# First scale and shift by quarters, and five products begun instead of three, in a decoder step of two layers

## The chip, the cores and the metric

One core of one Trainium2 chip. The metric is the device time of one execution in microseconds (us), the median of several runs. In the texts PE is TensorE, DVE is VectorE, ACT is ScalarE, POOL is GpSimd and SP is SyncE, which issues most DMAs.

## The reference, cut to what matters

Two layers of a decoder run for a prompt of 256 tokens and for 8 sample sequences of 4 tokens, 288 token columns in all, 1024 features. Each sub-layer starts with an RMSNorm that is scaled and shifted by vectors which a large product (`w_ada`) makes of a condition vector `c`:

```python
mod = cs @ p['w_ada'][l] + p['b_ada'][l]              # cs = silu(c), 1024 x 6144 weights a layer
sh1, sc1, g1, sh2, sc2, g2 = jnp.split(mod, 6, axis=-1)
xn = xf * lax.rsqrt(jnp.mean(xf * xf, axis=-1, keepdims=True) + EPS) * g
h = xn * (1.0 + scale[:, None, :]) + shift[:, None, :]
...
proj = jnp.einsum('btd,de->bte', h, w_in)             # retention: q, k, v, gate
q = rope(heads(q, RET_DK), pos0); k = rope(heads(k, RET_DK), pos0) * RET_DK ** -0.5
```

So nothing of the first layer's large product `h @ w_in` can start before `sh1` and `sc1`, that is before 8 MB of `w_ada` have arrived and been multiplied. All is float32; a product of the projections is made of three passes over weights and activations that are split into a high part and a low rest (`hi*hi`, `hi*lo`, `lo*hi`).

## The kernel before, in words

Features lie on partitions, tokens on columns; the 1024 features are 8 tiles of 128 (`KT`). Weights stream from memory in blocks of 128x1024 (512 KB) through SP's queue in the order that `plan_weights` writes down (L308); a block can be fetched when a place of its pool is free. A block of the projections is split on its way: ACT writes its high part (`whi`, L416), DVE the rest (`wlo`, L417), at most `LOOK` = 2 blocks ahead. A block of `w_ada` is used unsplit, by `ada_step` (L449): four matmuls of 32 columns of the array each. One output tile of the projection, called a product here, is 24 matmuls of 128x288 (3 passes times 8 feature tiles, `product`, L528). PE, DVE, ACT, POOL and SP each run a fixed order of instructions, which a scheduling layer makes when the program is built; an instruction that waits holds all that stand behind it on its engine.

The first phase is `first_h` (L659). `w_ada`'s first two chunks (`ada(0)`, `ada(1)`, 8 blocks each) are laid out so that the first chunk gives scale and shift of feature tiles 0 to 3 and the second of tiles 4 to 7. After the first chunk `modulated` (L612) makes h of tiles 0 to 3: on DVE scale times norm weight (`am`), the sample columns (`hs`, three steps), the prompt columns (`h`), on ACT the high part (`hh`, L637 and L646), on DVE the rest of the prompt columns (`hl`, L648). Then the first `EARLY` = 3 products are begun over tiles 0 to 3 (PSUM tiles `pe`), the second chunk's blocks lying between their weight blocks; when it is done, h of tiles 4 to 7 is made, and the three products are ended. Only then does `retention` go on: rotary positions on DVE (`rt`, L744 to L748) read the first four products, and the other products follow. The first phase has 8 places for blocks of its own (`RAW_START`) beside 4 common ones.

Constants of the first phase are fetched by ACT's queue: `cst_a` (cosines and sines, 288 KB), `cst_r` (902 KB), `cst_b`, `prm_b`. Each is held back by a copy of one column on POOL (`load_cst`, L521) that reads a scale or shift vector.

```python
            self.product(*begun[-1], KT, 0, P, h, 0, KT // 2)
        ...
        for i, (p, w) in enumerate(begun):
            if i == FREE:
                self.hold = False
            self.product(p, w, KT, 0, P, h, KT // 2)
```

## Time and profile before, and how to read them

| | |
|---|---|
| median of 3 runs | 1219.81 us (1219.09 to 1222.64) |
| the profiled execution's own time | 1217.6 us |
| its span in the profile | 1215.8 us |
| PE busy | 1150.0 us, 95% of the span |
| DVE, ACT, POOL busy | 872.7, 609.1, 316.2 us |
| DMA | 269 MB, mean 221 GB/s |
| granted PE clock, mean | 0.982 |

The profile shows one execution. The views used are: the page (busy time by engine), busy time by stretch with the granted clock and DMA, who waited for whom, and the timeline of one engine, whose rows give start, duration, engine, line, operation and, in brackets, an idle time and what ended it. A matmul on plain float32 operands shows as two records, one of the split parts as one; the rows of a timeline merge records of one form that follow each other, and the last record's drain is part of a row's duration, so that the pace is read from start to start.

### The profile page before, as it was taken

The page shows a single profiled execution, that of the slowest core. Times are in us where ns is not written, and L with a number is a line of the kernel's source. Part 1 is how long each engine was busy: PE and PEld are TensorE (multiplying, and loading weights), DVE is VectorE, ACT ScalarE, POOL GpSimd, SP SyncE. Part 2 cuts the span into 40 slices and gives each one's busy share as a digit, 9 for nine tenths or more (in the row PEclk, how much of TensorE's full clock was granted, in tenths as well). Part 3 has the DMA queues.
Part 4 walks back from the last instruction along what each step waited for, and adds up shares of the span by engine and source line. Part 5 has one row for each costly group of instructions (what it writes and reads, how often), then busy time and mean ns, then how long its engine had stood idle before and what let it go on. Part 6 is the DMA issues. An engine that isn't in the chain of part 4 may idle for free.

```text
span 1215.8 us, 24453 instructions
## 1 busy us (share of the span) xinstructions
PE 1150.0 (95%) x9236; PEld 1036.6 (85%) x9236; DVE 872.7 (72%) x2032; ACT 609.1 (50%) x1256; POOL 316.2 (26%) x496
## 2 busy tenths in 40 slices
PE   6999999999999999999888989998999899999996
PEld 2879798797869999998687878877889699999996
DVE  3657574664766666666778989896975687877785
ACT  2444534345346544453685656754544365555553
POOL 0213142150311222223242223332222212322232
PEclk9999999999999999999999999998999899999998
DMA  9998696876689656555727753544444987778521
GB/s 365 346 331 331 224 353 212 318 249 229 239 272 411 210 171 193 170 184 196 281 75 229 234 159 97 144 131 122 130 119 131 330 334 249 256 241 271 181 77 57
DMA packets 97477, 269.04 MB, mean 221 GB/s; under 512 B 26816, under 2 KB 29088, under 8 KB 97232
## 3 DMA queue, kind: packets, MB, share of 16 engines
q1 hardware_dynamic: 87456, 234.57, 57.5%
q0 software_dynamic: 8032, 29.16, 6.4%
q10 hardware_dynamic: 1872, 3.76, 0.9%
q8 instruction: 73, 1.20, 0.4%
q14 instruction: 44, 0.36, 0.1%
HBM read 236.06 MB, written 31.39 MB: 220 GB/s over the span
## 4 chain that ended last, share of the span: by engine, by line
PE 76%; DVE 13%; DMA 5%; ACT 3%; issue 2%; POOL 1%; SPq 0%; POOLq 0%; ACTq 0%; DVEq 0%
PE down L535 17%; PE fg L535 12%; PE fv L535 12%; PE pg L535 4%; PE pv L535 4%; PE adaP L455 4%; PE p L535 3%; PE gv L535 3%; DVE wlo L417 3%; DVE mp L1362 2%; PE pO L898 1%; PE pU L917 1%; DVE Ti L1366 1%; PE gk L535 1%; PE pe L1388 1%
## 5 line engine op out<-in xcount | busy, mean ns | idle before, releaser
L417 DVE TENSOR_TENSOR wlo<-more,whi 128x1024 fp32r<-128x1024 f32 x138 | 170.9, 1239 | 74.6 <-ACT whi L416 64.1
L416 ACT CAST whi<-more 128x1024 fp32r<-128x1024 f32 x138 | 144.3, 1047 | 136.9 <-PE down L535 51.6
L417 DVE TENSOR_TENSOR wlo<-raw,whi 128x1024 fp32r<-128x1024 f32 x123 | 155.4, 1267 | 65.3 <-ACT whi L416 48.9
L416 ACT CAST whi<-raw 128x1024 fp32r<-128x1024 f32 x123 | 128.1, 1045 | 134.1 <-PE down L535 32.5
L716 POOL TENSOR_TENSOR x<-x,dt 128x32 f32<-128x32 f32 x159 | 103.1, 650 | 135.0 <-DVE dt L714 134.2
L712 DVE SCALAR_TENSOR_TENSOR x<-down,mod,x 128x256 f32<-128x256 f32 x160 | 76.7, 480 | 50.7 <-PE down L535 50.0
L591 POOL TENSOR_TENSOR fal<-cv,fah 128x288 fp32r<-128x288 f32 x44 | 41.5, 943 | 215.8 <-ACT fah L590 173.9
L535 PE MATMUL down<-fal,whi 128*128 128x288 f32 x352 | 64.0, 294 | 0.0
L535 PE MATMUL down<-fah,whi 128*128 128x288 f32 x352 | 62.3, 294 | 0.0
L535 PE MATMUL down<-fah,wlo 128*128 128x288 f32 x352 | 62.1, 294 | 0.0
L535 PE MATMUL fg<-hh_ffn,whi 128*128 128x288 f32 x352 | 58.6, 299 | 1.2 <-ACT hh_ffn L637 1.2
L918 DVE SCALAR_TENSOR_TENSOR S<-S,pU 128x512 f32<-128x512 f32 x64 | 42.2, 685 | 24.1 <-PE pU L917 24.0
L535 PE MATMUL fv<-hh_ffn,whi 128*128 128x288 f32 x352 | 58.5, 298 | 0.0
L535 PEld LDWEIGHTS fg<-hh_ffn,whi 128*128 128x128 f32 x352 | 50.4, 189 | 5.6 <-ACT hh_ffn L646 2.6
L535 PE MATMUL fg<-hh_ffn,wlo 128*128 128x288 f32 x352 | 55.1, 296 | 0.0
L535 PE MATMUL fv<-hh_ffn,wlo 128*128 128x288 f32 x352 | 54.8, 295 | 0.0
L535 PE MATMUL fv<-hl_ffn,whi 128*128 128x288 f32 x352 | 54.3, 295 | 0.0
L535 PE MATMUL fg<-hl_ffn,whi 128*128 128x288 f32 x352 | 54.0, 295 | 0.0
L535 PEld LDWEIGHTS down<-fah,whi 128*128 128x128 f32 x352 | 51.8, 188 | 0.8 <-ACT whi L416 0.4
L535 PEld LDWEIGHTS down<-fal,whi 128*128 128x128 f32 x352 | 52.3, 188 | 0.2 <-issue 0.2
L535 PEld LDWEIGHTS fv<-hh_ffn,whi 128*128 128x128 f32 x352 | 50.3, 189 | 2.5 <-ACT ftail L947 1.6
L535 PEld LDWEIGHTS down<-fah,wlo 128*128 128x128 f32 x352 | 52.0, 188 | 0.0
(505 smaller groups left out, 2887.9 us busy)
## 6 DMA issues: line engine op xcount, KB each, us to landing
raw<-in_wada SPq DMA_DIRECT2D x69, 512.0 KB, 4.7
more<-in_wu SPq DMA_DIRECT2D x68, 512.0 KB, 4.9
raw<-in_wgi SPq DMA_DIRECT2D x48, 512.0 KB, 3.8
more<-in_wada SPq DMA_DIRECT2D x43, 512.0 KB, 5.8
more<-in_wd SPq DMA_DIRECT2D x41, 512.0 KB, 3.7
S<-in_sr SPq DMA_DIRECT2D x16, 1024.0 KB, 8.7
out_rs<-S POOLq DMA_DIRECT2D x16, 1024.0 KB, 7.2
raw<-in_wri SPq DMA_DIRECT2D x28, 512.0 KB, 4.8
```

The costliest lines, as they stand in the source:

```text
L416: nc.scalar.copy(hi[:, :c], r)
L417: nc.vector.tensor_tensor(lo[:, :c], r, hi[:, :c].bitcast(F32), ALU.subtract)
L455: nc.tensor.matmul(self.adaP[32 * g : 32 * g + 32, 0:256], lhsT=self.cs[:, k, :], rhs=rv[:, :, g, :], start=(k == 0), stop=(k == KT - 1), ...
L535: self.nc.tensor.matmul(out, lhsT=av[:, k, c0 : c0 + m], rhs=b[:, k, :], start=(k0 == 0 and i == 0), stop=(k1 == kts and i == len(seq) - 1))
L591: (nc.gpsimd if pool_lo else nc.vector).tensor_tensor(lo, src, hi.bitcast(F32), ALU.subtract)
L712: nc.vector.scalar_tensor_tensor(xm[:, :TP], p[:, :TP], g[:, 0:1], xm[:, :TP], ALU.mult, ALU.add)
L716: (nc.vector if gate == 11 and last and m == KT - 1 else nc.gpsimd).tensor_tensor(xv, xv, t, ALU.add)
L898: nc.tensor.matmul(pO4[32 * g : 32 * g + 32, :], lhsT=qm[:, c, 4 * bb + g, :], rhs=S[bb, c][:, g, :], start=(bb == 0 and c == 0), stop=Fal ...
L917: nc.tensor.matmul(pU, lhsT=kms[g][:, c * P : (c + 1) * P], rhs=vst, start=True, stop=True)
L918: nc.vector.scalar_tensor_tensor(S[bb, c][:, g, :], S[bb, c][:, g, :], gamma4, pU, ALU.mult, ALU.add)
L1362: nc.vector.tensor_tensor(m, Ti[:, 0:k, :].rearrange("p j c -> p c j").unsqueeze(1).to_broadcast([P, w, 8, k]), X[:, 0:k, i:k].rearrange(" ...
L1366: nc.vector.tensor_reduce(Ti[:, i:k, :], m, AX.X, ALU.add)
```

## The change

- Scale and shift of the first norm come by quarters of two feature tiles: `w_ada`'s first 16 blocks are laid out anew (`wadq`), four blocks a quarter; a quarter's matmuls have 128 columns instead of 256, eight a block instead of four (`ada_quarter`).
- `FIRST_W` = (1, 1, 3, 0): one product is begun after each of the first two quarters, three after the third, none after the fourth, five in all. Each quarter first continues the products that were begun.
- The begun products lie in PSUM banks of the tags `c`, `mm`, `s`, `mm`, `e`; the products that follow start the rotation `RET_TAGS` at its beginning, so the sixth product takes bank `c`, where the first lies.
- 15 places instead of 8 for the first phase's blocks.
- The four constants go through SP's queue behind the second and third block of the next phase, and nothing holds them.
- The first split of the next phase is issued behind the last instructions of h (`issue_after`); the first matmul of chunk 2 keeps its place in the program.

```diff
-EARLY = 3
-LATE = 1
+FIRST_W = (1, 1, 3, 0)
+EARLY = sum(FIRST_W)
+START_TAGS = ["c", "mm", "s", "mm", "e"]
 FREE = 1
-RAW_START = 8
+RAW_START = 15
...
-        second, step = ada(1), -(-KT // (EARLY - LATE))
-        plan = [ada(0)]
-        for i in range(EARLY):
-            plan[0] += wl("wri", i, 1) + second[i * step : (i + 1) * step]
+        plan = [[]]
+        for q, n in enumerate(FIRST_W):
+            plan[0] += [("ada", q - 4, k, A["wadq"][4 * q + k]) for k in range(4)]
+            plan[0] += wl("wri", sum(FIRST_W[:q]), n)
...
             n = self.order[self.n_dma]
+            self.late_cst.pop(n, lambda: None)()
...
+            with ExitStack() as behind:
+                if self.plan[n][4] and self.plan[n - 1][4] == 0:
+                    for i in self.first_end:
+                        behind.enter_context(self.tc.issue_after(i))
+                nc.scalar.copy(hi[:, :c], r)
+                nc.vector.tensor_tensor(lo[:, :c], r, hi[:, :c].bitcast(F32), ALU.subtract)
...
+            if ch == 2 and k == 0 and g == 0:
+                self.tc.keep_in_program_order(i)
...
+    def ada_quarter(self, q, k, r):
+        nc = self.nc
+        rv = r.rearrange("p (a g f) -> p a g f", a=2, g=4)
+        for a in range(2):
+            for g in range(4):
+                nc.tensor.matmul(
+                    self.adaP[32 * g : 32 * g + 32, 0:P], lhsT=self.cs[:, 2 * k + a, :], rhs=rv[:, a, g, :],
+                    start=(k == 0 and a == 0), stop=(k == 3 and a == 1), skip_group_check=True,
+                )
+        if k == 3:
+            ev = self.tmp.tile([P, T], F32, tag="t288", name="adaev", bufs=T288)[:, 0:P]
+            nc.scalar.copy(ev, self.adaP[:, 0:P])
+            pt = self.aux("adaT")
+            nc.tensor.transpose(pt[:, 0:P], ev, self.ident)
+            pt = pt[:, 0:P].rearrange("p (m r) -> p m r", r=32)[:, :, 0:9]
+            for m, m0 in ((0, 8 + 2 * q), (2, 2 * q)):
+                bias = self.prm("bada")[:, m0 : m0 + 2].unsqueeze(2).to_broadcast([P, 2, 9])
+                nc.vector.tensor_tensor(self.mod[:, m0 : m0 + 2, :], pt[:, m : m + 2], bias, ALU.add)
...
-        self.load_cst(rc, "cst_a", nc.scalar, self.mod[:, 8, 0:1])
...
+        n = next(i for i, b in enumerate(self.plan) if b[4])
+        sp = nc.sync
+        self.late_cst[n + 1] = lambda: self.load_cst(rc, "cst_a", sp)
+        self.late_cst[n + 2] = lambda: [self.load_cst(p, c, sp) for p, c in ((rc, "cst_r"), (self.cp, "cst_b"), (self.cp, "prm_b"))]
         begun = []
         self.hold = True
+        rb = None
+        for q, n in enumerate(FIRST_W):
+            self.ada_due()
+            if q == 0:
+                rb = self.now(self.token_rsqrt(self.ssum, 1.0 / DM, "ret"))
+            self.modulated(0, 0, 1, "ret", *h, rb, 2 * q, 2 * q + 2)
+            for i, (p, w) in enumerate(begun):
+                if q == 3 and i == FREE:
+                    self.hold = False
+                    self.advance()
+                self.product(p, w, KT, 0, P, h, 2 * q, 2 * q + 2)
+            for i in range(n):
+                w = self.weights("wri")
+                begun.append((self.aux(f"pe{len(begun)}", START_TAGS[len(begun)])[:, 0:T], w))
+                self.product(*begun[-1], KT, 0, P, h, 0, 2 * q + 2)
```

Where the instructions stand is seen in the orders of the two programs. The first place is PE around the last blocks of the first two chunks (`adaP` is their sum in PSUM, `adaT` its transpose, `pe_259`, `pe_295`, `pe_357` the three begun products). Before:

```order
L455 MATMUL adaP<-more_161,c 32x256
L535 MATMUL pe_295<-hh_ret,wlo 128x288 x4
L455 MATMUL adaP<-more_161,c 32x256 x3
L455 MATMUL adaP<-raw,c 32x256 x4
L455 MATMUL adaP<-more_169,c 32x256 x4
L455 MATMUL adaP<-more_195,c 32x256 x4
L464 MATMUL adaT<-cst,adaev 128x128 x2
L535 MATMUL pe_357<-hh_ret,whi 128x288 x4
```

And with the change, where `pe_259`, `pe_331`, `pe_417`, `pe_438`, `pe_457` are the five begun products and `raw`, `more_171`, `more_173` the fourth quarter's blocks:

```order
L567 MATMUL pe_417<-hh_ret,wlo 128x288 x6
L567 MATMUL pe_438<-hh_ret,whi 128x288
L567 MATMUL pe_438<-hl_ret,whi 128x288 x6
L567 MATMUL pe_438<-hh_ret,wlo 128x288 x6
L567 MATMUL pe_457<-hh_ret,whi 128x288 x2
L567 MATMUL pe_457<-hl_ret,whi 128x288 x6
L567 MATMUL pe_457<-hh_ret,wlo 128x288 x6
L488 MATMUL adaP<-raw,c 32x128 x16
L488 MATMUL adaP<-more_171,c 32x128 x8
L488 MATMUL adaP<-more_173,c 32x128 x8
L496 MATMUL adaT<-cst,adaev 128x128
L567 MATMUL pe_259<-hh_ret,whi 128x288
```

Before, eight matmuls of the third begun product's first half stay for after the transpose; with the change all of the third quarter's product matmuls stand ahead of the fourth quarter's blocks. Ahead of the twelve rows shown stand, in this order, one matmul of `pe_259` on `hl_ret`, two on `wlo`, one of `pe_331` on `hl_ret`, two on `wlo` and two of `pe_417` on `hl_ret`: 41 matmuls from that first one to the last before `adaP`.

The second place is DVE in the third quarter, with the change (`mod` in the last row is the fourth quarter's):

```order
L674 SCALAR_TENSOR_TENSOR h_ret<-x,am_ret,rb_ret 128x256
L668 TENSOR_TENSOR hs_ret<-hs_ret,mod 128x64
L425 TENSOR_TENSOR wlo<-more_144,whi 128x1024
L680 SCALAR_TENSOR_TENSOR hl_ret<-h_ret,mod,hh_ret 128x256
L674 SCALAR_TENSOR_TENSOR h_ret<-x,am_ret,rb_ret 128x256
L425 TENSOR_TENSOR wlo<-raw,whi 128x1024 x2
L680 SCALAR_TENSOR_TENSOR hl_ret<-h_ret,mod,hh_ret 128x256
L500 TENSOR_TENSOR mod<-adaT,prm 128x18 x2
```

The splits of the third, fourth and fifth block now stand between the pieces of h of the quarter's two tiles; the rest `hl_ret` of its second tile comes behind all three.

The third place is DVE at the end of the first phase. Before, the rotary steps (`rt`) of the first two products stand behind two splits:

```order
L648 SCALAR_TENSOR_TENSOR hl_ret<-h_ret,mod,hh_ret 128x256 x4
L417 TENSOR_TENSOR wlo<-more_203,whi 128x1024
L417 TENSOR_TENSOR wlo<-more_205,whi 128x1024
L744 TENSOR_TENSOR rt_423<-pe_259,cst_a 128x288
L745 TENSOR_TENSOR rt_424<-pe_259,cst_a 128x288
```

With the change they stand behind three, of the sixth to eighth block:

```order
L680 SCALAR_TENSOR_TENSOR hl_ret<-h_ret,mod,hh_ret 128x256 x2
L425 TENSOR_TENSOR wlo<-more_175,whi 128x1024
L425 TENSOR_TENSOR wlo<-more_179,whi 128x1024
L425 TENSOR_TENSOR wlo<-more_187,whi 128x1024
L775 TENSOR_TENSOR rt_581<-pe_259,cst_a 128x288
L776 TENSOR_TENSOR rt_582<-pe_259,cst_a 128x288
```

Before, the first product after the begun ones takes a bank that is free; with the change it is the sixth product, and it takes the bank that `rt_581` and `rt_582` read.

## Rows read from the trace of the kernel before

**Rows 1.** The page's first part: busy time, share of the span and instructions of each engine.

```profile
PE 1150.0 (95%) x9236; PEld 1036.6 (85%) x9236; DVE 872.7 (72%) x2032; ACT 609.1 (50%) x1256; POOL 316.2 (26%) x496
```

**Rows 2.** Busy time by stretch: start and end in us from the span's start, length, then busy us and instructions of PE, PEld, DVE, ACT and POOL, the granted PE clock, the share of DMA and GB/s.

```profile
8.00:20.00 12.00, 11.04 (x76) 4.61 (x75) 4.04 (x15) 1.33 (x4) 0.00 (x0) 1.00 1.03 411
22.00:24.28 2.28, 0.00 (x1) 0.01 (x1) 2.28 (x6) 0.81 (x2) 0.00 (x0) 1.00 0.94 258
24.28:26.00 1.72, 1.69 (x11) 0.71 (x11) 1.72 (x6) 1.29 (x3) 0.45 (x1) 1.00 1.01 394
26.00:28.00 2.00, 2.00 (x12) 0.74 (x14) 1.47 (x3) 1.07 (x2) 0.00 (x0) 0.53 1.03 399
28.00:30.00 2.00, 2.00 (x18) 0.95 (x11) 0.40 (x1) 0.00 (x0) 0.00 (x0) 0.62 1.04 416
36.00:40.00 4.00, 2.65 (x16) 2.19 (x17) 3.81 (x12) 1.58 (x5) 1.01 (x4) 1.00 1.02 409
46.00:100.00 54.00, 53.94 (x414) 46.40 (x413) 32.95 (x54) 24.37 (x43) 12.52 (x14) 1.00 0.94 341
100.00:340.00 240.00, 240.00 (x1763) 207.31 (x1762) 154.19 (x271) 106.01 (x181) 74.07 (x92) 1.00 0.74 262
```

**Rows 3.** Who waited for whom on PE from 8 to 44.6 us: engine, tile and line, what it waited for, us in total, times, the longest.

```profile
PE pe L535 <- ACT hh_ret L637: 2.7, 1, 2.7
PE adaT L464 <- ACT adaev L461: 1.0, 2, 0.5
PE pe L535 <- DVE wlo L417: 0.9, 1, 0.9
```

**Rows 4.** PE's timeline in the first 52 us.

```profile
7.88 1.08 PE L455 MATMUL adaP<-more,c 128*32 128x256 f32 x8 [7.88 <-DMA more<-in_wada]
...
11.89 1.08 PE L455 MATMUL adaP<-more,c 128*32 128x256 f32 x8 [0.20 <-DMA more<-in_wada]
13.17 1.06 PE L455 MATMUL adaP<-more,c 128*32 128x256 f32 x2 [0.20 <-DMA more<-in_wada]
14.16 1.44 PE L566 MATMUL st_ret<-ones,ssum 128*128 128x1 f32 x6
...
17.43 1.49 PE L575 MATMUL rb_ret<-cst,tr_ret 128*128 128x128 f32 x6
...
24.28 0.40 PE L535 MATMUL pe<-hh_ret,whi 128*128 128x288 f32 x1 [2.66 <-ACT hh_ret L637]
24.61 0.64 PE L455 MATMUL adaP<-raw,c 128*32 128x256 f32 x8
...
33.67 1.24 PE L455 MATMUL adaP<-more,c 128*32 128x256 f32 x15
...
39.47 1.60 PE L535 MATMUL pe<-hh_ret,whi 128*128 128x288 f32 x10
...
44.58 1.21 PE L535 MATMUL p<-hh_ret,whi 128*128 128x288 f32 x8
45.63 1.23 PE L535 MATMUL p<-hl_ret,whi 128*128 128x288 f32 x8
...
47.77 1.23 PE L535 MATMUL pv<-hh_ret,whi 128*128 128x288 f32 x8
...
50.97 1.23 PE L535 MATMUL pv<-hh_ret,whi 128*128 128x288 f32 x8
```

**Rows 5.** DVE's timeline: the root of the norm, h after the second chunk, splits, and rotary steps.

```profile
15.64 0.16 DVE L547 TENSOR_SCALAR rsv_ret<-st_ret 128x3 f32<-128x3 f32 x1 [4.54 <-PE st_ret L566]
...
17.21 0.16 DVE L557 SCALAR_TENSOR_TENSOR tr_ret<-rsu_ret,tr_ret 128x3 f32<-128x3 f32 x1
...
35.87 0.30 DVE L468 TENSOR_TENSOR mod<-adaT,prm 128x36 f32<-128x36 f32 x2 [7.46 <-PE adaT L464]
36.10 0.20 DVE L618 SCALAR_TENSOR_TENSOR am_ret<-mod,prm 128x36 f32<-128x36 f32 x1
36.33 0.29 DVE L628 TENSOR_TENSOR hs_ret<-x,am_ret 128x128 f32<-128x128 f32 x1
36.65 0.29 DVE L632 TENSOR_TENSOR hs_ret<-hs_ret,rb_ret 128x128 f32<-128x128 f32 x1
36.86 0.48 DVE L642 SCALAR_TENSOR_TENSOR h_ret<-x,am_ret,rb_ret 128x256 f32<-128x256 f32 x1
37.25 1.22 DVE L417 TENSOR_TENSOR wlo<-more,whi 128x1024 fp32r<-128x1024 f32 x1
...
44.78 0.46 DVE L744 TENSOR_TENSOR rt<-pe,cst_a 128x288 f32<-128x288 f32 x1 [0.33 <-PE pe L535]
45.16 0.45 DVE L745 TENSOR_TENSOR rt<-pe,cst_a 128x288 f32<-128x288 f32 x1
```

**Rows 6.** ACT's timeline around the second chunk's end.

```profile
22.59 0.51 ACT L646 ACTIVATE hh_ret<-h_ret,mod 128x256 fp32r<-128x256 f32 x1 [1.08 <-DVE h_ret L642]
...
34.97 0.37 ACT L461 COPY adaev<-adaP 128x256 f32<-128x256 f32 x1 [7.82 <-PE adaP L455]
35.24 1.05 ACT L416 CAST whi<-more 128x1024 fp32r<-128x1024 f32 x1
```

**Rows 7.** PE's timeline in a later layer, at matmuls of 32 columns of the array and 128 columns of data, the form that the change uses for `w_ada`'s first 16 blocks.

```profile
641.82 0.85 PE L1512 MATMUL pks<-gS,kqm 128*32 128x128 f32 x22
```

More of the change, by code (lines that the diff above doesn't have):

```diff
@@ L50 @@
 AHEAD = 2
-CST_AT = 4
 TASKS = ("gdn_solves", "gdn_inverses", "gdn_scores_all", "gdn_samples_all", "gdn_decays_all")
@@ L202, in lay_out @@
     wa = np.concatenate([inp["w_ada"][0], inp["w_ada"][1], inp["w_ada_final"]], 1)
-    wa[:, : 2 * DM] = wa[:, : 2 * DM].reshape(DM, 2, 2, 512)[:, ::-1].transpose(0, 2, 1, 3).reshape(DM, 2 * DM)
-    d["wada"] = wa.reshape(KT, P, 14, 1024).transpose(2, 0, 1, 3).reshape(14 * KT, P, 1024)
+    d["wada"] = wa[:, 2 * DM :].reshape(KT, P, 12, 1024).transpose(2, 0, 1, 3).reshape(12 * KT, P, 1024)
+    w = wa[:, : 2 * DM].reshape(4, 2, P, 2, 4, 256)[:, :, :, ::-1]
+    d["wadq"] = w.transpose(4, 0, 2, 1, 3, 5).reshape(16, P, 1024)
     parts = {
@@ L310, in plan_weights @@
         A = self.A
-        ada = lambda ch: [("ada", ch, k, A["wada"][ch * KT + k]) for k in range(KT)]
+        ada = lambda ch: [("ada", ch, k, A["wada"][(ch - 2) * KT + k]) for k in range(KT)]
         wl = lambda name, i0, n: [("w", name, 0, A[name][i]) for i in range(i0, i0 + n)]
@@ L370, in plan_weights @@
         self.n_dma = self.n_prep = self.n_use = 0
-        self.raw, self.split = {}, {}
+        self.raw, self.split, self.late_cst = {}, {}, {}
         self.extra, self.held = {}, {"raw": 0}
@@ L452, in ada_step @@
             self.adaP = self.aux("adaP", self.ada_tag)
+        if ch < 0:
+            return self.ada_quarter(ch + 4, k, r)
         rv = r.rearrange("p (c g f) -> p c g f", c=2, g=4)
         for g in range(4):
-            nc.tensor.matmul(
+            i = nc.tensor.matmul(
                 self.adaP[32 * g : 32 * g + 32, 0:256], lhsT=self.cs[:, k, :], rhs=rv[:, :, g, :],
@@ L465, in ada_step @@
             pt = pt[:, 0:256].rearrange("p (m r) -> p m r", r=32)[:, :, 0:9]
-            for m, m0, n in ((0, 8 + 4 * ch, 4), (4, 4 * ch, 4)) if ch < 2 else ((0, 8 * ch, 8),):
-                bias = self.prm("bada")[:, m0 : m0 + n].unsqueeze(2).to_broadcast([P, n, 9])
-                nc.vector.tensor_tensor(self.mod[:, m0 : m0 + n, :], pt[:, m : m + n], bias, ALU.add)
+            m0, n = 8 * ch, 8
+            bias = self.prm("bada")[:, m0 : m0 + n].unsqueeze(2).to_broadcast([P, n, 9])
+            nc.vector.tensor_tensor(self.mod[:, m0 : m0 + n, :], pt, bias, ALU.add)
+    def ada_quarter(self, q, k, r):
[16 more added lines that the diff above has]
+                nc.vector.tensor_tensor(self.mod[:, m0 : m0 + 2, :], pt[:, m : m + 2], bias, ALU.add)
     def spawn(self, gen):
@@ L614, in modulated @@
         nc = self.nc
-        n, ms = m1 - m0, slice(m0, m1)
+        n, ms, rb_given = m1 - m0, slice(m0, m1), rb
         am = self.tmp.tile([P, KT, 9], F32, tag="am", name=f"am_{name}", bufs=2)[:, 0:n]
@@ L645, in modulated @@
             else:
-                nc.scalar.activation(hi[:, m, :TP], h, AF.Identity, bias=shift[:, i, 0:1])
+                ends = [nc.scalar.activation(hi[:, m, :TP], h, AF.Identity, bias=shift[:, i, 0:1])]
             if lo is not None:
-                nc.vector.scalar_tensor_tensor(lo[:, m, :TP], h, shift[:, i, 0:1], hi[:, m, :TP].bitcast(F32), ALU.add, ALU.subtract)
-        self.ada_due(FILLS[2])
+                ends.append(nc.vector.scalar_tensor_tensor(lo[:, m, :TP], h, shift[:, i, 0:1], hi[:, m, :TP].bitcast(F32), ALU.add, ALU.subtract))
+        if rb_given is None:
+            self.ada_due(FILLS[2])
+        self.first_end = [i.ins for i in ends]
     def h_tiles(self, name):
```

22 lines of the change are left out of this document (removed).

## The prediction

> **What bounds the kernel now.** The page first: PE is busy 95% of the span [rows 1]. That alone says nothing about the first phase, so the second view is busy time by stretch: from 46 to 340 us PE has no gap [rows 2], so whatever the first phase takes off or adds before the product stream starts goes through to the end one for one. Third, PE's waits in the first 44.6 us, and fourth its timeline, which puts them in place: h of tiles 0 to 3 ends a wait of 2.66 us at 24.28, the last `adaP` matmul ends at 34.91, the ending of the three products starts at 39.47 and is over at 44.58, where the fourth product starts [rows 3, 4]. From there a product takes 3.19 us (44.58 to 47.77), so five products are done, and the sixth starts, at 50.97 [rows 4]. **This is the mark: when does the sixth product start with the change?** DMA is full (411 GB/s) in this phase [rows 2], so products that are done while `w_ada` arrives would be a gain. Whether more of them are is a question of the order on PE, and I walk that order with the rows' durations.
>
> **Landings.** SP's order in the change is 4 blocks of quarter 1, 1 product block, 4, 1, 4, 3, 4. A block is 0.524 MB, 1.28 us at 411 GB/s, and the fifth block of the old order, in the same place, is used at 13.17 [rows 4]: so block n lands at 13.2 + 1.28 (n - 5). Quarters 1 to 4 are complete at 11.9, 18.3, 24.7 and 33.7, the fifth product block at 28.5. With 15 places nothing holds this. The four constants (1.5 MB, 3.7 us) and three further product blocks follow, the last by 41.2; the first reader of a constant is the rotary step, far behind. Their move from ACT to SP and POOL's four copies cost nothing: ACT loses four issues, SP only issues here, and POOL has 1.0 us of work in 36 to 40 [rows 2]. Should they be late after all: `cst_a` lands at about 36 and is read at 54.
>
> **Quarter 1.** ACT takes the split of block 5 (landed 13.2, 1.05 us) ahead of the copy of the sum (0.37) [rows 6], so the transpose is at 14.6 and the norm's sums behind it run 15.1 to 16.5 (1.44) [rows 4]. The root took 1.73 us, 15.64 to 17.37 [rows 5]; two small steps (0.2 each) now stand between: 18.7. Its broadcast takes 1.49 [rows 4], then one sample step, `h` 0.48 and `hh` 0.51 [rows 5, 6]: first product matmul at 21.4, against 24.28.
>
> **A quarter's chain.** After the second chunk: 34.91 end of `adaP`, 35.87 `mod`, `h` done at 37.34, `hh` 0.5 later: 3.0 us if no split stands between; a split on DVE adds 1.22 [rows 4 to 6]. The sample steps have half the columns; 0.29 for 128 columns bounds them above, and I leave them there (at 0.2 each the chain is 0.2 shorter).
>
> **Quarter 2.** Its matmuls lie between product 1's first six and end at 22.7. `wlo` of the second block stands inside the chain: first `hh` at 22.7 + 3.0 + 1.2 = 26.9. Sixteen product matmuls (0.133 each, 24 in 3.19) with `hl` 0.9 behind end at 29.2. Then 19 matmuls of quarter 3, whose data landed by 24.7: the form's row gives 22 records in 0.6 us from start to start, 28 ns, two a matmul, so 1.1 us [rows 7]; the 256-column form needs 63 a matmul at least [rows 4], which would be 1.2. End 30.3.
>
> **Quarter 3.** `h` of its first tile ends at 30.3 + 2.4; then DVE has `hs`, `wlo` (1.22), `hl` (0.48), `h` (0.42), two `wlo`, `hl` [rows 5]: 0.2 + 1.2 + 0.5 + 0.4 + 2.4 + 0.5 = 5.2 more, 37.9. PE fills part of it with some 25 product matmuls, but behind that last `hl` stand 41, 5.5 us: 43.4. **Only now come the fourth quarter's matmuls**, which landed at 33.7: 32 of them, 1.8 us, 45.2.
>
> **Quarter 4.** No split inside its chain (they are issued behind): 48.2. Then six matmuls for each of five products, 4.0 us: 52.2. PE does nothing in the chain's 3.0 us, because every other begun matmul is done.
>
> **The sixth product.** It needs the first one's bank, read by two rotary steps that stand on DVE behind three splits. ACT's last `hh` is at 49.4; one split on ACT 1.05, then three on DVE 3.7: 54.1; two rotary steps, 0.38 from start to start and 0.45 for the last [rows 5]: 55.0. Behind the waiting product on PE stands everything, so this stall counts in full.
>
> **The sum.** 55.0 - 50.97 = +4.0 us. Removed: one of two long chains' waits and half the ending. Added: 64 more matmuls at the same total PE time, two more chains, each with PE partly idle.
>
> **The clock.** After the stretch 22.00 to 24.28 without a matmul the granted clock is 0.53 and 0.62 in the four us from 26.00, the 1.2 GHz level for most of them; after 36 to 40, with PE busy 2.65 of 4 us, it stays at 1.00 [rows 2]. That loss is 2 x 0.47 + 2 x 0.38 = 1.7 us of PE work. The changed walk has thinly filled stretches at 22.7 to 26.9, around 31 to 34, and 45.2 to 48.2. One such fall costs from 0 (it lies in a wait) to 1.7; I take 1.0, since PE's work is on the path in about half of 21.4 to 48.2 (1.3 + 3.4 + 7.3 of 26.8 us). The Trainium skill (TensorE: Matmul & The Clock Gate, HAM oscillation) says that waits between bursts put the array back to its low rate, each time anew. The trace agrees at 26, and not after 36 to 40. By the rule alone all three stretches would count, up to 3 x 1.7 = 5.1 us: the last rival below.
>
> So +5.0: 1217.6 + 5.0 = 1222.6 for the profiled execution, which lies 2.2 below the median of the runs shown; **against the median, 1224.8 us**. The forecast's own range is +3.5 to +6.5, 1223.3 to 1226.3. A measurement of this kernel can tell 0.3%, 3.7 us, from no change: below 1216.2 is faster, above 1223.5 slower.
>
> **Rivals.**
>
> *No change: DVE's chains are overpriced.* If the third quarter's last `hl` came at 35.5 instead of 37.9, the 41 matmuls end at 41, and if the three splits ran under the last 30 matmuls, the sixth product starts at 50.5 to 53: -0.5 to +2, and 1219 to 1222 us. For it: the sample steps are shorter than I price them, and the order has no other wait. Against it: the splits, 1.05 and 1.22, make most of the chain and are measured many times. Chance 0.23.
>
> *Not slower, by PE.* The fourth quarter's blocks lie in SBUF from 33.7, when PE is waiting on DVE. If PE took these matmuls ahead of product matmuls that wait, they would be over at about 38.4, `hh` at 41.4, and the 41 + 30 product matmuls would run without a break from 38.4, 9.5 us, to 47.9; splits and rotary steps would be done by then (42.3 + 1.05 + 3.7 + 0.8 = 47.9): -3.1, 1216.7; with shorter sample steps 1214. It decides if `adaP` of the last blocks is seen before 40 us. Against it: at 24.28 PE waited 2.66 us with `adaP` matmuls right behind that ran 0.33 us after [rows 4]. The same page of the Trainium skill (Part 2, What happens when you issue a matmul) speaks of a reorder window, but for weight loads alone; matmuls stay in order. The trace shows nothing else. Chance 0.13.
>
> *The clock falls more than once.* Two or three falls, each followed by product matmuls on the path, cost 1.7 each: +7 to +10, 1227 to 1230. For it: three thin stretches instead of one. Against it: 36 to 40. Chance 0.15.
>
> The forecast itself: 0.49. That the change doesn't do what it says is not among them: the orders show quarters, five begun products and the constants on SP.
>
> **How the numbers follow.** Faster comes only from PE's rival and its better half, 0.10. Same takes the rival of no change and the rest of PE's, 0.26, and a sliver of the forecast that ends below 1223.5, 0.02: 0.28. Slower: the rest, 0.62. The range for 8 in 10 leaves out the rival of PE (0.13) and the end of the clock's (0.05): from 1218.5 to 1229.
>
> **What would show it right or wrong.** First product matmul near 21.4. `adaP` of the last four blocks at 43 to 46, though their DMAs landed by 34. A PE wait of 2 to 3 us on ACT's `hh` before the last six matmuls of each product. `wlo` three times between the last `hl` and the first rotary step, and a PE wait of 1.5 to 3 us on DVE at the sixth product, which starts near 55. Beyond 60 us the same stream, shifted. Wrong, if the sixth product starts before 51, or if PE has gaps between 60 and 340 us, which this walk doesn't have.

## The result, and the profile after

The changed kernel took **1231.84 us** (median of 8 runs, 1227.53 to 1237.02) against 1218.28 of the kernel before on the same chip (8 runs, 1213.08 to 1222.64): ratio **1.0107, 95% interval 1.0084 to 1.0131**, 13.6 us slower. The forecast was 1224.8, its range 1218.5 to 1229: the sign was right, the size not. As a difference it was +5.0, from a median of 1219.81 over three runs of the kernel before, against 13.6 measured. The profiled execution is the slowest of the eight, 1237.02 us, 19.4 us over the profiled one of before; below, points inside the traces are compared, and their sums with the medians.

The first part of the page after, the answer to [rows 1]: 128 records more, which are 64 matmuls, and PE's share is no higher.

```profile
PE 1164.5 (94%) x9364; PEld 1050.2 (85%) x9364; DVE 874.4 (71%) x2044; ACT 608.0 (49%) x1260; POOL 310.3 (25%) x494
```

PE's timeline of the changed kernel at the points that the walk named (start, busy us; in brackets the wait before it and what ended that).

```profile
20.78 0.61 PE L567 MATMUL pe<-hh_ret,whi 128*128 128x288 f32 x1 [0.37 <-ACT hh_ret L669]
...
29.09 0.85 PE L567 MATMUL pe<-hh_ret,whi 128*128 128x288 f32 x2 [0.52 <-ACT hh_ret L678]
...
30.85 0.44 PE L567 MATMUL pe<-hl_ret,whi 128*128 128x288 f32 x1
31.09 0.44 PE L567 MATMUL pe<-hh_ret,whi 128*128 128x288 f32 x1
31.33 0.68 PE L567 MATMUL pe<-hl_ret,whi 128*128 128x288 f32 x2
...
38.78 3.54 PE L567 MATMUL pe<-hh_ret,whi 128*128 128x288 f32 x13 [0.72 <-ACT hh_ret L669]
...
48.72 1.08 PE L488 MATMUL adaP<-raw,c 128*32 128x128 f32 x32
49.62 1.06 PE L488 MATMUL adaP<-more,c 128*32 128x128 f32 x32
51.12 0.33 PE L496 MATMUL adaT<-cst,adaev 128*128 128x128 f32 x1 [0.44 <-ACT adaev L494]
53.58 0.93 PE L567 MATMUL pe<-hh_ret,whi 128*128 128x288 f32 x5 [2.14 <-ACT hh_ret L669]
...
59.29 1.30 PE L567 MATMUL pv<-hh_ret,whi 128*128 128x288 f32 x8 [1.46 <-DVE rt L776]
```

The shape is the walk's: the first product matmul at 20.78 (walk 21.4), the fourth quarter's 64 matmuls behind all products of the third, a wait of 2.14 us for its `hh`, and a wait of 1.46 us for the rotary step at the sixth product. What is off is how fast PE gets there: product matmuls start every 0.24 us at 31 (half pace, below), where the kernel before needs 0.13 (full pace). At 29.09 PE is 2.2 us behind the walk, at 48.72 5.3, at the sixth product 4.3 (59.29 for 55.0). Against 50.97 [rows 4] the sixth product is **8.3 us late, not 4.0**.

DVE's timeline in front of that wait: three splits, then the rotary steps.

```profile
54.91 3.50 DVE L425 TENSOR_TENSOR wlo<-more,whi 128x1024 fp32r<-128x1024 f32 x3 [0.45 <-ACT whi L424]
58.33 0.45 DVE L775 TENSOR_TENSOR rt<-pe,cst_a 128x288 f32<-128x288 f32 x1
58.69 0.45 DVE L776 TENSOR_TENSOR rt<-pe,cst_a 128x288 f32<-128x288 f32 x1
```

So the sixth product is 4.3 us later than the walk had it, and 3.3 later than the forecast, which added 1.0 for the clock.

Behind the sixth product the loss grows. The sums for the first feed-forward wait for the last head of retention; before, then after:

```profile
343.96 0.83 PE L566 MATMUL st_ffn<-ones,ssum 128*128 128x1 f32 x6 [0.54 <-DVE ssum L610]
```

```profile
358.66 0.83 PE L598 MATMUL st_ffn<-ones,ssum 128*128 128x1 f32 x6 [0.54 <-DVE ssum L642]
```

14.7 us: 8.3 at the mark, and **6.4 between it and here**, where PE shows no other wait. From here to the end the time varies from execution to execution: 871.1 to 876.5 us in three traces of the changed kernel, 864.0 to 872.3 in the kernel before and its edited forms. So two things were to be explained: 4.3 us more than the walk at the mark, and 6.4 behind it where the forecast had none.

### The profile page after: what moved, and what is told of

Same layout as the page of the kernel before. It is cut to its first block, busy times and chain, and to the rows that moved or that the text cites. A ratio compares the mean times of both kernels' runs of the same rounds, so it can differ in the third digit from the quotient of the medians.

```text
span 1235.2 us, 24725 instructions
## 1 busy us (share of the span) xinstructions
PE 1164.5 (94%) x9364; PEld 1050.2 (85%) x9364; DVE 874.4 (71%) x2044; ACT 608.0 (49%) x1260; POOL 310.3 (25%) x494
## 4 chain that ended last, share of the span: by engine, by line
PE 77%; DVE 12%; DMA 5%; ACT 3%; issue 2%; POOL 1%; SPq 0%; POOLq 0%; ACTq 0%; DVEq 0%
PE down L567 17%; PE fg L567 12%; PE fv L567 11%; PE pg L567 4%; PE pv L567 4%; PE adaP L465 3%; PE p L567 3%; PE gv L567 3%; DVE wlo L425 2%; DVE mp L1393 2%; PE gk L567 2%; PE pO L929 2%; PE pU L948 2%; PE pe L567 1%; PE pS L899 1%
## 5 line engine op out<-in xcount | busy, mean ns | idle before, releaser
L425 DVE TENSOR_TENSOR wlo<-more,whi 128x1024 fp32r<-128x1024 f32 x139 | 170.5, 1229 | 82.2 <-ACT whi L424 67.7
L425 DVE TENSOR_TENSOR wlo<-raw,whi 128x1024 fp32r<-128x1024 f32 (+1 forms) x122 | 152.6, 1254 | 63.4 <-ACT whi L424 44.9
L424 ACT CAST whi<-raw 128x1024 fp32r<-128x1024 f32 (+1 forms) x122 | 126.9, 1044 | 136.1 <-PE down L567 38.6
L747 POOL TENSOR_TENSOR x<-x,dt 128x32 f32<-128x32 f32 x159 | 98.4, 620 | 133.9 <-DVE dt L745 133.2
L623 POOL TENSOR_TENSOR fal<-cv,fah 128x288 fp32r<-128x288 f32 x44 | 40.7, 924 | 217.5 <-ACT fah L622 172.9
L567 PE MATMUL fg<-hh_ffn,whi 128*128 128x288 f32 x352 | 58.5, 299 | 0.7 <-ACT hh_ffn L669 0.7
```

What stands on the lines that cost most here:

```text
L424: nc.scalar.copy(hi[:, :c], r)
L425: nc.vector.tensor_tensor(lo[:, :c], r, hi[:, :c].bitcast(F32), ALU.subtract)
L567: self.nc.tensor.matmul(out, lhsT=av[:, k, c0 : c0 + m], rhs=b[:, k, :], start=(k0 == 0 and i == 0), stop=(k1 == kts and i == len(seq) - 1))
L623: (nc.gpsimd if pool_lo else nc.vector).tensor_tensor(lo, src, hi.bitcast(F32), ALU.subtract)
L747: (nc.vector if gate == 11 and last and m == KT - 1 else nc.gpsimd).tensor_tensor(xv, xv, t, ALU.add)
```

## Experiments

All times in us. "Sixth" is the start of the sixth product in the run's trace, "ffn" that of the sums for the first feed-forward, both less the same point of the kernel before (50.97 and 343.96). The ratio is to the kernel before on the same chip, whose medians were 1217.2, 1217.0, 1217.5 and 1219.5 in the four groups. Single executions have no interval; those of `a_bnka2` and `a_bnka3` ran on another chip, where one execution of the kernel before took 1222.1. The intervals of most edits of the changed kernel overlap, so what one edit is worth is read from the traces.

| run | edit | median | ratio (95%) | sixth | ffn |
|---|---|---|---|---|---|
| after | the change | 1231.8 | 1.0107 (1.0084 to 1.0131) | +8.3 | +14.7 |
| a_again1, 2 | none, single executions | 1231.2, 1232.9 | | +8.1, +7.7 | +14.2, +13.8 |
| a_nmm | count of products 5 | 1226.0 | 1.0078 (1.0057 to 1.0098) | +8.0 | +9.5 |
| a_q4 | quarter 4 among quarter 3's products | 1225.3 | 1.0084 (1.0051 to 1.0117) | +5.7 | +9.9 |
| a_q4nmm | both | 1225.3 | 1.0069 (1.0043 to 1.0094) | +5.2 | +6.2 |
| a_bnka | both, sixth product in bank a | 1223.6 | 1.0040 (1.0016 to 1.0065) | -0.1 | +1.3 |
| a_bnka2, 3 | the same, single executions | 1218.1, 1228.5 | | +1.4, +3.4 | +3.1, +5.1 |
| a_warm | 21 idle matmuls | 1229.8 | 1.0105 (1.0084 to 1.0125) | +9.6 | +12.9 |
| a_three | three begun, count as before | 1223.6 | 1.0050 (1.0022 to 1.0079) | +3.6 | +3.8 |
| a_threeq4 | a_three, quarter 4 as in a_q4 | 1222.2 | 1.0024 (1.0000 to 1.0048) | +5.3 | +6.0 |
| b_rot | before, count shifted by 3 | 1221.9 | 1.0040 (1.0017 to 1.0063) | -0.1 | +4.4 |
| b_rot2 | before, count shifted by 2 | 1216.5 | 0.9993 (0.9967 to 1.0018) | +1.1 | +1.4 |
| b_cst | before, places and constants | 1217.5 | 1.0008 (0.9986 to 1.0029) | -0.1 | -1.5 |
| b_warm | before, 18 idle matmuls | 1217.7 | 0.9996 (0.9974 to 1.0019) | +0.3 | +0.7 |
| b_five | before, five begun | 1224.0 | 1.0051 (1.0028 to 1.0075) | +5.4 | +5.5 |
| b_fivel | b_five, weights asked for later | 1221.7 | 1.0014 (0.9993 to 1.0035) | +2.7 | +3.2 |

### The phase of the bank cycle

The kernel before takes its three begun products through `mmt`, which counts them; the change takes five through `aux`, which doesn't. So the count stands at 0, not 5, when the sixth product asks for its bank, and every product of the retention has another bank than before. `a_nmm` puts the count right:

```diff
         self.hold = False
+        self.n_mm = EARLY
         self.begun = [p for p, _ in begun]
```

> The changed kernel with one line more: the count of products is set to five after the first phase, so that the sixth product and all behind it use the PSUM banks that the same products use in the kernel before (sixth in a bank of the pair, instead of the bank that the rope still reads). Theory (the mark's parts add up): the 1.46 us that the sixth product waited for its bank at 57.8 to 59.3 us go, the rest stays: 1230.3 us against 1231.8 of the changed kernel, ratio to the kernel before about 1.010. Rival (the rotation of banks through the whole retention is what costs the 5 us between the mark and the first feed-forward): 1225 to 1226 us, and the second head's statistics no longer fall behind by more than at the mark.

Measured: the sixth product still waits (2.19 us, now for the rotary step that reads another bank), and the distance of the medians to the kernel before shrinks from 13.6 to 8.8, at the first feed-forward from 14.7 to 9.5. That was the rival's number. The intervals of the two ratios overlap, the traces differ clearly. The test from the other side puts the shift alone into the kernel before; `b_rot2` has 2 in place of 3:

```diff
-        self.mm_tags, self.n_mm = RET_TAGS, 0
+        self.mm_tags, self.n_mm = RET_TAGS, 3
```

> The kernel before with one number changed: the count of products starts at 3 instead of 0, so that the products of the retention go through the four banks of their cycle in the changed kernel's phase (sixth product in the bank c instead of one of the pair); nothing else of the change is in it. Theory (the phase of the bank cycle sets the order in which products and side tasks are laid on TensorE, and this order is worse by 4 to 6 us over the four heads): start of the sixth product as before within 0.5 us, statistics of the first feed-forward 4 to 6 us later, 1222 to 1224 us against 1217 to 1219. Rival (the phase is harmless; the run with the count set to five was faster for another reason, or by its order alone): within 1.5 us of the kernel before.

> The kernel before with the count of products starting at 2 instead of 0: the banks c and s trade places in the cycle, so the first of each pair of rope products stays in c or s as in the kernel before, and the pairs of the other products too. Theory (what costs is which products of a head share c and s with the retention's side tasks; a swap of the two alone is nearly harmless): sixth product within 0.5 us, statistics of the first feed-forward within 1.5 us, 1216 to 1219 us. Rival (any phase but the one that the kernel before has costs 4 us): 1221 to 1223 us. Second rival (this phase is better): below 1215 us.

PE's timeline of `b_rot` at the sixth product and at the feed-forward's sums:

```profile
50.85 1.23 PE L535 MATMUL pv<-hh_ret,whi 128*128 128x288 f32 x8
...
348.34 0.83 PE L566 MATMUL st_ffn<-ones,ssum 128*128 128x1 f32 x6 [0.54 <-DVE ssum L610]
```

The same start, 4.4 us lost by the feed-forward, 4.9 at the median (2.1 to 7.7 by the interval): **one number that the diff changes by the way costs 4 to 5 us**. The shift by 2, where `c` and `s` only trade places, has a ratio of 0.9993 and loses 0.35 us behind its sixth product, though that product came 1.1 us late, where 0.5 at most was expected.

The table says the same for all traces (ffn less sixth): the six in the changed kernel's phase (`after`, `a_again1`, `a_again2`, `a_q4`, `a_warm`, `b_rot`) lose 3.3 to 6.4 us between the two points, the twelve others -1.4 to +1.7. Repeats of one kernel agree within 0.35 us there.

One wait of `b_rot` is seen, and it is 1.6 of the 4.4:

```profile
258.42 1.32 PE L535 MATMUL p<-hh_ret,whi 128*128 128x288 f32 x8 [1.57 <-ACT whi L416]
```

ACT came late to that split since it had waited 10.33 us for a store to give its buffer back, as its own timeline in `b_rot` shows:

```profile
256.83 0.59 ACT L870 COPY so<-pS 128x512 f32<-128x512 f32 x1 [10.33 <-DMA out_rp<-so]
257.32 2.00 ACT L416 CAST whi<-raw 128x1024 fp32r<-128x1024 f32 x2
```

The rest is spread over PE's order. For instance `adaP` between the sixth product and the feed-forward (the last row of busy time by stretch for this tile alone: length of the stretch, PE's busy us) in `after`, `a_nmm`, `b_rot` and the kernel before:

```profile
sum 299.37, PE 20.13; mean PE 20.13
```

```profile
sum 294.50, PE 17.07; mean PE 17.07
```

```profile
sum 297.49, PE 19.51; mean PE 19.51
```

```profile
sum 292.99, PE 18.07; mean PE 18.07
```

The same 234 records take 1.4 us more in `b_rot` than in the kernel before, and 3.1 more in `after` than in `a_nmm`; `b_rot2`, which loses almost nothing, has 18.70. The order differs too: between the two points PE's timeline has the `down` products in 22 separate pieces in `after`, `a_again1`, `a_q4`, `a_warm` and `b_rot`, and in 13 to 16 in the kernel before, `a_nmm`, `a_q4nmm`, `a_bnka`, `a_three`, `b_rot2`, `b_cst` and `b_warm`. Why this order costs PE more without a wait in the records stays open.

### The clock in the first phase

> The changed kernel with 21 matmuls on the tile of ones into an unused bank (added work with no use): 20 before the first block lands, one behind the third block. Theory (the half pace from 8 to 34 us is a clock that starts late, and it costs): product matmuls between 20 and 34 us start every 0.13 us instead of 0.24, 3 us, and if the granted 0.5 to 0.6 at 38 to 42 us goes as well, 2 us more: 1227 to 1229 us. Rival (in that stretch the landings, ScalarE and VectorE set the time, TensorE's pace doesn't): 1231 to 1232 us. Second rival (the extra work draws the throttle earlier or more often): 1233 to 1236 us.

The 21 idle matmuls of `a_warm` are 18 at the start and 3 in the first quarter; `b_warm` has the 18 alone.

```diff
         if k == 3:
+            if q == 0:
+                self.warm(3)
...
+    def warm(self, n):
+        w = self.aux("warm", "e")
+        for i in range(n):
+            self.nc.tensor.matmul(w[:, 0:P], lhsT=self.ones, rhs=self.ones, start=True, stop=True)
...
         rb = None
+        self.warm(18)
```

> The kernel before with 18 matmuls on the tile of ones into an unused bank ahead of the first scale-and-shift block (added work with no use). In the changed kernel the like of it moved the sixth product by +1.3 us and brought no gain. Theory (in the first 24 us landings, ScalarE and VectorE set the time, not TensorE's pace): 1216 to 1220 us, sixth product within 1 us of 50.97. Rival (the early clock pays where the order is not disturbed, as it is not here): sixth product 1 to 2 us earlier, 1215 to 1217 us.

Neither decides it. `a_warm`'s median, 1229.8, lies between its theory and its rival; `b_warm`'s, 1217.7, is in its theory's range. In `a_warm` the sums of the norm moved, PE waited 1.95 us for the root, the half pace came back at 52.58 to 58.5, and the sixth product is later; in `b_warm` the sixth product is within 0.3 us of the kernel before. The added work changed the pattern, it did not hold the pace.

> The changed kernel once more, unaltered, for one look: does its first phase run at the same pace from one execution to the next? Theory (the half pace from 20 to 34 us of the profiled run is a matter of the single execution, as the run with another count of products, whose order on TensorE is the same up to the sixth product, suggests: it had full pace from 21.3 to 26 us and reached the last hh 1.6 us earlier against the start of its first block): the last hh of the fourth quarter between 51.5 and 53.6 us where the first block starts at 7.9, and the sixth product between 57.5 and 59.5. Rival (the pace belongs to the order of work): within 0.3 us of the first look, 53.58 and 59.29.

> The changed kernel a third time, one look, for the same question: same numbers as for the look before; behind the mark both theories expect the first feed-forward's statistics 5 to 7 us later against the kernel before than the sixth product was.

The fourth quarter's last `hh` came at 52.33 and 52.94, the sixth product at 59.10 and 58.64. All four lie inside the theory's bounds, as do the first trace's own times, and only 59.10 within the rival's 0.3 us. Yet both executions ran at half pace from 20 to 32 as the first one; they differ behind it, where `after` is slow again at 39 to 42 and `a_again1` at 54 to 57. Busy time in one stretch (as in [rows 2]; the granted clock is the third number from the end) shows how little the clock column says of it. `after`, then `a_again1`:

```profile
28.00:32.00 4.00, 3.48 (x22) 2.36 (x16) 1.77 (x5) 1.15 (x3) 0.32 (x1) 1.00 1.03 410
```

```profile
28.00:32.00 4.00, 3.48 (x17) 2.68 (x15) 1.35 (x4) 0.91 (x2) 0.32 (x1) 0.50 1.03 410
```

One pace, 0.24 us from matmul to matmul in both, and the granted clock reads 1.00 in one and 0.50, the 1.2 GHz level, in the other: in `after` only the spacing shows it, and that the clock was low there too is inferred from the equal spacing.

The clean test came with `a_bnka` (below), whose PE order up to the sixth product is that of `a_q4nmm`. It has three traces, the first from one chip and the other two from another.

> The kernel with the fourth quarter's matmuls among the third quarter's products, the count set to five and the sixth product in the bank a, unaltered, for one look more. Theory (the pace of the first phase belongs to the single execution): another pattern of full and half pace than the first look's (full throughout), and the sixth product then 2 to 5 us later than 50.86, as much as the matmuls at half pace add. Rival (the pace belongs to the kernel): full pace again from 20 us on and the sixth product within 0.5 us of 50.86.

> The same a third time, for the same question and with the same numbers.

PE's timeline in the three, at the first block, at the third quarter's `hh` and at the sixth product; in the first also two rows that show the full pace, 0.13 us from start to start:

```profile
7.82 1.08 PE L488 MATMUL adaP<-more,c 128*32 128x128 f32 x16 [7.82 <-ACT sq L638]
...
28.24 0.30 PE L567 MATMUL pe<-hl_ret,whi 128*128 128x288 f32 x1
28.37 0.30 PE L567 MATMUL pe<-hh_ret,whi 128*128 128x288 f32 x1
...
34.23 0.67 PE L567 MATMUL pe<-hh_ret,whi 128*128 128x288 f32 x3 [0.72 <-ACT hh_ret L669]
...
50.86 1.21 PE L567 MATMUL pv<-hh_ret,whi 128*128 128x288 f32 x8
```

```profile
7.90 1.08 PE L488 MATMUL adaP<-more,c 128*32 128x128 f32 x16 [7.90 <-ACT sq L638]
...
35.70 0.66 PE L567 MATMUL pe<-hh_ret,whi 128*128 128x288 f32 x3 [0.72 <-ACT hh_ret L669]
...
52.33 1.21 PE L567 MATMUL pv<-hh_ret,whi 128*128 128x288 f32 x8
```

```profile
7.86 1.08 PE L488 MATMUL adaP<-more,c 128*32 128x128 f32 x16 [7.86 <-ACT sq L638]
...
37.15 3.64 PE L567 MATMUL pe<-hh_ret,whi 128*128 128x288 f32 x13 [0.72 <-ACT hh_ret L669]
...
54.33 1.21 PE L567 MATMUL pv<-hh_ret,whi 128*128 128x288 f32 x8
```

The granted clock of 28 to 32 and of 36 to 40 in the same three:

```profile
28.00:32.00 4.00, 3.57 (x55) 3.04 (x53) 0.06 (x1) 0.55 (x2) 0.00 (x0) 1.00 1.03 411
...
36.00:40.00 4.00, 3.97 (x48) 2.93 (x48) 2.29 (x3) 0.48 (x2) 0.00 (x0) 1.00 1.02 400
```

```profile
28.00:32.00 4.00, 4.00 (x39) 3.41 (x42) 0.13 (x1) 0.00 (x0) 0.00 (x0) 0.68 1.03 410
...
36.00:40.00 4.00, 3.69 (x34) 2.65 (x33) 3.76 (x6) 1.95 (x3) 0.42 (x1) 1.00 1.02 398
```

```profile
28.00:32.00 4.00, 4.00 (x19) 3.57 (x18) 0.12 (x1) 0.00 (x0) 0.00 (x0) 0.50 1.03 410
...
36.00:40.00 4.00, 3.28 (x15) 2.84 (x14) 4.00 (x8) 2.95 (x5) 0.70 (x1) 0.64 1.02 399
```

**One kernel, one order, starts within 0.08 us, and the sixth product at 50.86, 52.33 or 54.33**: from 20 us on no fall of the clock, one, or two. The price of the clock in this phase is 0, 1.5 or 3.5 us. The last two ran on one chip, so the chip does not make the difference between them.

None of the three traces of `after` was free of it, and their low stretch is longer. All these traces begin at half pace: a block's 16 `adaP` records take 1.08 us, and 0.64 at full pace. `a_nmm` and the three of `a_bnka` go over to full pace at about 20 us; from there the second and third of `a_bnka` fall as said. `after`, `a_again1` and `a_again2` are at half pace from 20 to 33. Yet the order on PE up to the third quarter's `hh` is the same in all of them, and `a_nmm` ran on the chip of `a_again1` and `a_again2`. So the price of that one stretch can be read directly: `a_again2`, which is at full pace from 35 us on, reaches the same `hh` **4.1 us later** than `a_bnka` (38.36 for 34.23, its first block 0.10 later). Its rows:

```profile
38.36 0.67 PE L567 MATMUL pe<-hh_ret,whi 128*128 128x288 f32 x3 [0.71 <-ACT hh_ret L669]
...
58.64 1.29 PE L567 MATMUL pv<-hh_ret,whi 128*128 128x288 f32 x8 [1.46 <-DVE rt L776]
```

What makes one execution leave the low pace, or fall back to it, and another not stays open.

### Which part of the order costs

```diff
             self.modulated(0, 0, 1, "ret", *h, rb, 2 * q, 2 * q + 2)
+            if q == 2:
+                self.load()
+                self.ada_early(4)
```

> The changed kernel with the fourth quarter's 64 scale-and-shift matmuls offered to TensorE already while the third quarter's products are written down, so that they stand among those products instead of behind all 41. Theory (the fourth quarter's chain is late because its matmuls wait in TensorE's order behind 8 us of products, though landed 14 us before): the matmuls still take their 1.9 us, the chain of 3.0 us lies beside products: 1228.8 us against 1231.8, and TensorE's wait of 2.1 us for the last hh goes. Rival (the time of the first phase is set by TensorE's pace and its sum of work, the chain only fills what is idle): 1231 to 1232 us. Second rival (what is won here is lost again behind the mark): the mark comes 3 us earlier and the time is the same.

> The changed kernel with both edits: the fourth quarter's matmuls among the third quarter's products, and the count of products set to five behind the first phase. Theory (the two act in different places, 2.6 us at the mark and some 5 us between the mark and the first feed-forward): 1220 to 1222 us, 3 to 4 us over the kernel before, and the statistics of the first feed-forward 5 to 6.5 us behind those of before. Rival (both gain the same lost time): 1224 to 1226 us.

PE's wait of 2.14 us for the fourth quarter's `hh` is gone, as expected. The distance of the medians fell from 13.6 to 8.1, more than the 3.0 expected, though the intervals overlap, and with the count put right as well to no less than 8.3: the sum of the two gains, 1220 to 1222, did not come at the median, which lies in the rival's range, though at the first feed-forward it did (+6.2 in place of +14.7). `a_q4nmm`'s trace has half pace at 27 to 33 and again at 37 to 40.7. What the place of the matmuls is worth is read between traces of one pace: `a_nmm` and `a_q4nmm` reach the third quarter's 13 `hh` matmuls at 37.66 and 37.11 and take 3.61 and 3.64 us for them; their sixth products are at 58.95 and 56.18, 2.77 apart, less 0.55: **2.2 us**. `a_q4` and `a_again2`, which have the count of the changed kernel and full pace from there on, take 17.78 (38.87 to 56.65) and 20.28 us (38.36 to 58.64) from that `hh` to the sixth product: 2.5 us.

```diff
-            p = self.mmt(name)[:, 0:T]
+            p = (self.aux(name, "a") if self.n_mm == EARLY else self.mmt(name))[:, 0:T]
+            self.n_mm += self.n_mm == EARLY
```

> The changed kernel with the fourth quarter's matmuls among the third quarter's products, the count set to five, and the sixth product in the bank a, which the scale-and-shift matmuls leave at about 49 us, instead of one that the rope has to read first. Theory (the wait of about 1 us in front of the sixth product is one for its bank alone): that wait goes, products up to the first gate product 1 us earlier, 1 us less than the kernel without the edit: 1224 us. Rival (the seventh product waits for the rope instead, since VectorE's splits of the next weights stand ahead of the rope): sixth product earlier by 1 us, first gate product not, same time, 1225 us.

Bank `a` is free when the last `adaP` has been copied out, so the sixth product need not wait for the rope. Here the third trace of `a_bnka` has `a_q4nmm`'s pace (37.15, 3.64 us): 54.33 against

```profile
56.18 1.28 PE L567 MATMUL pv<-hh_ret,whi 128*128 128x288 f32 x8 [1.74 <-DVE rt L782]
```

That is 1.9 us less, 1.5 at the first gate product: the wait was one for the bank, and the rope did not come back at the seventh, as the theory had it. In the changed kernel, whose sixth product follows the second rotary step and not the fourth (1.46 in place of 2.19 us in `a_nmm`), the same should be worth 1.2 by subtraction. The traces agree: at full pace `a_q4` takes 17.78 us from the third quarter's `hh` to the sixth product and `a_bnka` 16.63 (34.23 to 50.86), 1.15 apart.

> The changed kernel with three begun products instead of five (one in each of the first three quarters), and banks from the fourth product on as in the kernel before: quarters, places and constants as changed. Theory (what costs is that four chains of quarters replace two of halves, each with its fixed part on VectorE and ScalarE): 1230 to 1232 us. Rival (the two more begun products cost, by the wait of the fourth quarter behind their matmuls and by the bank of the sixth): 1221 to 1224 us.

Here `FIRST_W = (1, 1, 1, 0)` and the count is set to 3. The rival's time came, 1223.6 against 1226.0 of `a_nmm`, in overlapping intervals. But its trace has the full clock at 36 to 42, so its +3.6 and the 4.4 to `a_nmm` hold some clock as well.

> The quartered kernel with three begun products, and the fourth quarter's scale-and-shift matmuls offered to TensorE among the third quarter's products. Theory (most of the 3.6 us that quarters cost at the mark is the fourth chain, in which TensorE waits 2.1 us for hh and holds 34 of 64 matmuls, 1.3 us, ahead of it): sixth product 2 to 3 us earlier than with three begun products alone, 0.6 to 1.6 us behind before, 1218 to 1221 us. Rival (the 3.6 us are the four chains' work on VectorE and ScalarE, wherever TensorE's matmuls stand): sixth product at most 1 us earlier, 1222 to 1224 us.

Inconclusive: the median is in the rival's range, but the sixth product came later (+5.3), as this trace is at half pace from 20 to 34 and `a_three`'s only around 30; the intervals of the two ratios overlap.

```diff
-EARLY = 3
-LATE = 1
+EARLY = 5
+LATE = 2
+START_TAGS = ["c", "mm", "s", "mm", "e"]
...
-            begun.append((self.mmt(f"pe{i}")[:, 0:T], w))
+            begun.append((self.aux(f"pe{i}", START_TAGS[i])[:, 0:T], w))
```

> The kernel before with five begun products instead of three, halves kept (three ahead of the second half's chain, two behind it; fifteen places; the constants as before, on ScalarE's queue), banks of the five as in the changed kernel and the cycle's phase behind them as before. Theory (two more begun products cost by the sixth product's wait for a bank that the rope reads, 1 to 2.2 us in the runs so far, and by nothing else): sixth product 1 to 2.5 us later than 50.97, 1218 to 1220 us. Rival (five begun products cost 4 to 5 us at the mark as they do between the quartered kernels with three and with five): sixth product 4 us later or more, 1221 to 1223 us. Second rival (they gain, since the second half's matmuls and its chain lie beside more products): sixth product earlier than 50.5, 1215 us or less.

> The kernel before with five begun products as in the run with halves, but with the weights of the third to fifth product asked for behind all blocks of the second half instead of the third's ahead of two of them. Theory (one block more ahead of the second half's last, 1.3 us of landing at 410 GB/s, makes its chain late, and that is 1.3 to 2 us of the 4.4): first gate product 2.4 to 3.1 us behind before, 1220 to 1222 us. Rival (the chain's splits and the low clock set it, not the landing): 4 us behind or more, 1224 us.

Both also have 15 places and the count set to five; in `b_fivel` the step of the second half's blocks is 4 for `-(-KT // (EARLY - LATE))`. Five begun products cost the kernel in halves 1.0051 too, as the rival of `b_five` had it, and its wait for the bank is only 0.65 us of that. Asking for the third weight behind the second half's blocks gives 2.8 us at the sixth product back, since the transpose of that half starts at 36.68 in place of 39.16; more than the 1.3 to 2 that I had expected, at a median in the theory's range. `b_five` also shows a granted clock of 0.50 at 42 to 44, so some of the 2.8 may be the clock's. In halves and in quarters alike, five begun products in place of three gained nothing.

> The kernel before with one part of the change alone: fifteen places for the first blocks instead of eight, and the constants of the first phase in SyncE's order instead of behind modulated values on ScalarE's queue; halves and three begun products as before. Theory (this part hides behind the landings, as the prediction had it): sixth product within 0.7 us of 50.97, 1217 to 1220 us. Rival (its transfers delay the blocks of the first product, or the fourth product now begins among the begun ones and waits): sixth product 1 to 3 us later, 1220 to 1223 us. Second rival (without held constants the kernel before gains): 1215 us or less.

The diff is the change's own lines on `late_cst` and `RAW_START`. The sixth product at 50.84, ratio 1.0008: places and constants cost nothing, as the walk had it.

## Why the prediction was wrong

- **The walk of the order held.** First product matmul, order of the quarters, wait for `hh`, three splits ahead of the rope, wait at the sixth product: all seen. No trace of the changed kernel has full pace throughout, but its time there can be put together from two: `a_bnka`, in the same order up to the third quarter's `hh`, reaches it at 34.23, and `a_again2` takes 20.28 us from there to the sixth product. Together 54.5, +3.5, for the walk's 55.0 and +4.0. Of it, 2.5 is the place of the fourth quarter's matmuls and 1.15 the bank.
- **The clock's term was mis-sized.** I took +1.0 for one fall (0 to 1.7). The three traces of the changed kernel are 7.7 to 8.3 late; less 3.5, that is 4.1 to 4.8 us. Most of it (4.1 in `a_again2`) is the low pace from 20 to 34 us, for which the walk had nothing: it priced every product matmul at 0.133, the kernel before's pace behind its mark [rows 4]. The rival of more than one fall (+7 to +10 at the mark) got 0.15 and has the right size at the mark, but only in part the right cause: in `after` and `a_again2` the long stretch had lasted since the first block and is no fall behind a thin stretch, and in `a_again2` it is the only one. The Trainium skill (TensorE: Matmul & The Clock Gate, HAM oscillation) names waits between bursts, each time anew, and by it the prediction had up to 5.1 us. The size is near, by another way; and `a_bnka`'s trace with 50.86 had the same waits in the same places as its other two and no fall, so here the waits allow it and do not set it.
- **"Beyond 60 us the same stream, shifted" failed.** 6.1 to 6.4 us (ffn less sixth in three traces) were lost there, where the sum had nothing. `b_rot` shows 4.5 from the count of products alone (ffn less sixth), and `a_nmm`, with the count put right, has 1.5 left, whose cause stays open. The walk read the new bank of the sixth product from the diff and did not ask what bank every later product gets, though the line that takes the begun products out of the count stands in the diff.
- **Sum.** 3.5 + 4.5 + 6.2 = 14.2 at the feed-forward (means of the three traces), against 13.6 between the medians. The three add up to the traces by construction, as the second is what the first leaves of the lateness at the mark; what supports them are the comparisons above: at one pace for the first, in one order for the second, and from both sides for 4.5 of the third.
- **No change, and PE ahead of itself**: both fell. DVE's chains were hardly overpriced: 48.72 to 53.58 is 4.9 us for the fourth quarter, the walk's 4.8, and the third quarter's last `hl` ends 7.0 us behind its `adaP`, for the walk's 7.6, where the rival needed 2.4 less. PE took nothing ahead of a waiting matmul: the last four blocks' `adaP` runs at 48.72.
- One aside of the walk is misread: 63 ns for the 256-column form is the time of a record, and a matmul has two. The sum does not use it.
- None of these kernels is measurably faster than the kernel before. The best with five begun products in quarters is `a_bnka`, 1.0040, the best with three `a_threeq4`, 1.0024.

## What to carry to other kernels

When a change takes work out of a rotating counter, follow the counter to the end of the phase that uses it: the shift of a bank cycle alone cost 4 to 5 us here, as much as the whole forecast. Walk a short, thinly filled phase twice, once at full pace and once at the low pace, and give the range both ends; a single trace shows one draw. To price one wait, compare traces that reach the point before it at the same pace.

## What was not expected of the hardware

- The same order went from 20 us to its sixth product with no, one or two stretches at the lower clock (50.86, 52.33, 54.33 us), with the first block's start within 0.08 us.
- The column of the granted clock read 1.00 over 20 to 34 us in two of three traces of the changed kernel while matmuls of 288 columns started every 0.24 us, and 0.50 from 20 to 32 in the third at the same spacing: read the spacing beside the column.
